# Two RG-LRU pairs around a chunked RWKV-7 recurrence: later places for convolutions, gate products and the second pair, state sums in PSUM, one square on ScalarE

## The chip, the core and the metric

The kernel runs on one core of a Trainium2 chip. The metric is the time of one execution on the device in microseconds, the median of several runs. One further execution is recorded by the hardware profiler; its rows are what the text below reads. Engines are named PE (TensorE; PEld its weight loads), DVE (VectorE), ACT (ScalarE), POOL (GpSimd) and SP (which here issues nearly all DMAs).

## The reference, cut to what matters

Two layers over 512 tokens and a model width of 1024. Each layer projects the normed input once and feeds three mixers, whose gated outputs are concatenated, projected and added to the residual. Two mixers matter here. RWKV-7 carries a 64 x 64 state per head (8 heads) along the tokens; the RG-LRU is a causal convolution of four taps, two gates from 64 x 64 blocks, and an elementwise linear recurrence. The third mixer, latent attention (MLA), follows after both.

```python
# rwkv7_mix, per token
sa = einsum('bhij,bhj->bhi', S, kk_t)
S = S * w_t[:, :, None, :] - sa[..., None] * b_t[:, :, None, :] + v_t[..., None] * k_t[:, :, None, :]
y_t = einsum('bhij,bhj->bhi', S, r_t)
# rglru_mix
xc = conv_b + sum(up[:, j:j + T] * conv_w[j] for j in range(4))
gate_r = sigmoid(xb @ ga_w + ga_b); gate_i = sigmoid(xb @ gx_w + gx_b)
log_a = -8.0 * gate_r * softplus(-lam); a = exp(log_a)
bx = sqrt(-expm1(2.0 * log_a)) * (gate_i * xc)
h_t = a_t * h_{t-1} + bx_t          # then rms_norm over the 512 channels
```

## The kernel before

Channels lie on the 128 partitions, tokens along the free axis, so each 512-wide mixer is four blocks of 128 channels. A projection block (`proj`, L331) is 24 matmuls of 128 x 128 x 512: fp32 weights and inputs are each split in two fp32r halves, and three of the four products are summed (`mm3`, L232). `weights` (L217) loads a raw half-block (`wr`, 3 buffers), ScalarE copies its high part (`wH`, 4 buffers), and VectorE or GpSimd subtracts to get the low part (`wL`, 4 buffers, L229): VectorE takes every `wmod`-th half, GpSimd the others. `wmod` is set by the stages; in the stretch of the change it is 2 (`WB`).

RWKV-7 is computed in eight chunks of 64 tokens (`chunk`, step `H`). Chunk `ch` multiplies the state by prepared matrices (L849, 16 matmuls into `ck`), adds the result to the values `UV` on VectorE (L852, two halves), multiplies values by keys (L859, 16 matmuls into `so` in PSUM), and makes the next state on VectorE: sum with the old state (L863), times the decay (L864); in chunk 0 only the product (L866). Every second chunk also makes outputs (L877, L883), copies them (L885, VectorE), squares them (L886, ScalarE) and reduces them (L887, VectorE). The eight chunks are a serial chain between TensorE and VectorE; matmuls of projections that don't depend on it can stand between its steps.

The RG-LRU blocks 0 and 1 are prepared before the chunks, 2 and 3 between them. `lru_a` (step `A`) projects a block, copies it with a margin (`ub`) and scales it (`xc`, L679) on ScalarE, adds three taps on VectorE (L681), multiplies by the gate blocks on TensorE (L687) and applies sigmoids and a tanh. `lru_b` (step `B`) takes a pair of blocks: exponential on ScalarE, `a` squared on GpSimd (L702), two VectorE operations (L704, L705), root on ScalarE, a product on GpSimd (L710), the scan on VectorE (L712), squares (L716, L718), their sum on GpSimd (L719), and the gated output on VectorE (L720). `B0` stands before the chunks, `B1` is called after them.

The order of calls is written by hand in strings (`ORD1` to `ORD3`). It is a priority, not the order on an engine: the framework plans each engine's fixed order of instructions ahead of time from the calls and from its own estimate of when operands are ready, so an instruction of a later call can stand before one of an earlier call. `act` (L133) chains all table functions of ScalarE in the order of the calls. Tiles of one tag share a fixed number of buffers: `g2` (128 x 512 floats) has 11, the projection accumulators `acc` four PSUM banks. After the chunks come `N0` (group norm), output gates `g`, latent projections `t` (four accumulators at once, `lat_products` L901), `T` (latents), `R0` (token sums of the RG-LRU, L379 on TensorE), `Y0` (split of its outputs), then output projections and attention.

Of the kernel before, what the change touches and what calls it, by code (L numbers as in the profile page):

```python
# [1 line left out]

# [9 lines left out]
AF = mybir.ActivationFunctionType  # L12
# [4 lines left out]
T = 512  # L17
# [30 lines left out]
def body(ctx, tc, x, wc, wl, wo, w2a2, gagx, wuq, wukv, vec, ln_g, fin_g, cst, out, depth=DEPTH):  # L48
# [11 lines left out]
    BN = (2, 2, 0, 0)  # L60
    ORD1 = "M0 L0 L1 C0 M1 C1 P0 L2 O0 M2 U1 O1 C2 U2 P1 L3 M3 C3 U0 P2 O2"
    ORD2 = "G0 U3 G1 P3 G2 Z0 Z1 O3 G3 X0 f4 V0 V1 Z2 Q0 Q1 f0 V2 V3 f1 Q2 Q3 J0 f2 J1 K0 f3 W0 K1 W1 f5 W2 W3"
    ORD3 = "B0 H0 H1 A2 H2 H3 A3 H4 H5 H6 H7 B1 N0 g0 g1 t0 t6 t1 t2 t4 t5 t3 t7 T0 R0 Y0 g2 g3 T1"
    LO = "0ig12uw3yvcm"
    Q1 = "aoooottttaaaooookvvqvkqvkqkqqqqq"
    WA, WB, WC, WD, WF = 1000, 2, 2, 5, 1000

    def tl(tag, shape, dt=F32, bufs=1):
        cnt[0] += 1
# [2 lines left out]
    def g2(shape=(128, 512)):  # L72
        return tl("g2", shape, F32, bufs=11)
# [16 lines left out]
    def ps(shape=(128, 512)):  # L90
        cnt[0] += 1
        return PS.tile(list(shape), F32, tag="ps", name=f"ps_{cnt[0]}", bufs=2)
# [40 lines left out]
    def act(out, in_, func, **kw):  # L133
        st = {AF.Sigmoid: "S", AF.Tanh: "S", AF.Sqrt: "Q"}.get(func, "E")
        if cur[0] != st:
            chained(A.preload_act_table_set(SETS[st]))  # L136
            cur[0] = st
        chained(A.activation(out=out, in_=in_, func=func, **kw))  # L138

    def copy(out, in_, **kw):  # L140
        i = A.activation(out=out, in_=in_, func=AF.Copy, **kw)  # L141
        return getattr(i, "ins", i)
# [178 lines left out]
    def one_layer(l):  # L321
        def vc(n, j):
            o = VO[n] + j
            return vecs[:, l, o:o + 1]
# [6 lines left out]
        def proj(j, halves=False):  # L331

            if halves:
                o = acc()
                W = [weights(wc[l, j, :, 4 * hf:4 * hf + 4, :].rearrange("p k c -> p (k c)"), raw=raws.pop((j, hf), None)) for hf in range(2)]
                for th in range(2):
                    t = slice(th * 256, (th + 1) * 256)
                    for k in range(8):
                        s = slice((k % 4) * 128, (k % 4 + 1) * 128)
                        w = W[k // 4]  # L340
                        mm3(o[:, t], (w[0][:, s], w[1][:, s]), (xH[:, k, t], xL[:, k, t]), k == 0, k == 7)
                return o
            o, parts = proj_parts(j)
            for part in parts:
                part()
            return o
# [320 lines left out]
        gw = tl("w2", [128, 2, 4, 64])  # L667
        nc.sync.dma_start(out=gw, in_=gagx[l])

        st = {}  # L670

        def lru_a(*js, o=None):
            for j in js:
                o = o or proj(17 + j)
                ub = g2([128, T + 3])
                G.memset(ub[:, 0:3], 0.0)
                copy(ub[:, 3:], o)
                xc = g2()
                A.activation(out=xc, in_=o, func=AF.Identity, scale=vc("cw", 12 + j), bias=vc("cb", j))  # L679
                for t in range(3):  # L680
                    V.scalar_tensor_tensor(out=xc, in0=ub[:, t:t + T], scalar=vc("cw", 4 * t + j), in1=xc, op0=ALU.mult, op1=ALU.add)  # L681
                gt = []
                for w in range(2):
                    o = ps()
                    for e in range(2):
                        hr = slice(64 * e, 64 * e + 64)
                        PE.matmul(o[hr, :], gw[hr, w, j, :], xc[hr, :], start=True, stop=True)  # L687
                    s = g2()
                    act(s, o, AF.Sigmoid, bias=vc("gx_b" if w else "ga_b", j))
                    gt.append(s)  # L690
                G.tensor_tensor(out=gt[1], in0=gt[1], in1=xc, op=ALU.mult)
                th = g2()
                act(th, gt[0], AF.Tanh, scale=sp8[:, l, j:j + 1])
                st[j] = (gt[0], gt[1], th)
                o = None

        def lru_b(*js):
            for j in js:
                a, bx, th = st[j]
                act(a, a, AF.Exp, scale=nsp8[:, l, j:j + 1])  # L700
                a2 = g2()
                G.tensor_tensor(out=a2, in0=a, in1=a, op=ALU.mult)  # L702

                V.scalar_tensor_tensor(out=a2, in0=a2, scalar=1.0, in1=th, op0=ALU.add, op1=ALU.mult)  # L704
                V.tensor_scalar(out=a2, in0=a2, scalar1=1.0e-34, scalar2=None, op0=ALU.max)  # L705
                st[j] += (a2,)
            for j in js:
                a, bx, th, a2 = st[j]
                act(a2, a2, AF.Sqrt)
                G.tensor_tensor(out=bx, in0=bx, in1=a2, op=ALU.mult)  # L710
                hs = th
                V.tensor_tensor_scan(out=hs, data0=a, data1=bx, initial=0.0, op0=ALU.mult, op1=ALU.add)  # L712
                sq = a2
                if j == 0:
                    stb[0] = tl("sqn", [128, T])
                    A.activation(out=stb[0], in_=hs, func=AF.Square)  # L716
                else:
                    A.activation(out=sq, in_=hs, func=AF.Square)  # L718
                    G.tensor_tensor(out=stb[0], in0=stb[0], in1=sq, op=ALU.add)  # L719
                V.scalar_tensor_tensor(out=hs, in0=hs, scalar=vc("out_g", j), in1=gz[j], op0=ALU.mult, op1=ALU.mult)  # L720
                yb.append(hs)
# [119 lines left out]
        def chunk(ch):  # L841
            cp, par = ch // 2, ch % 2
            ur = slice(64 * (1 - par), 64 * (1 - par) + 64)
            if ch:
                uo = [ck([128, 4, 64]) for _ in range(2)]
                for p in range(4):
                    for e in range(2):
                        hr = slice(64 * e, 64 * e + 64)
                        PE.matmul(uo[e][ur, p, :], AR[p][hr, 0, ch * 64:(ch + 1) * 64], S[ch][hr, p, :], start=True, stop=True)  # L849
                for e in range(2):  # L850
                    u = UV[ur, :, ch, 64 * e:64 * e + 64]
                    V.tensor_tensor(out=u, in0=uo[e][ur, :, :], in1=u, op=ALU.add)  # L852
            if ch < 7:
                so = ck([128, 4, 64])
                for p in range(4):
                    for e in range(2):
                        hr = slice(64 * e, 64 * e + 64)
                        hc = slice(e * 64, (e + 1) * 64)
                        PE.matmul(so[hr, p, :], BT[p][:, ch, hc], UV[:, p, ch, hc], start=True, stop=True)  # L859
                sn = S[ch + 1] = tl("S", [128, 4, 64], bufs=3)  # L860
                pc = PC[:, :, ch:ch + 1].to_broadcast([128, 4, 64])
                if ch:
                    V.tensor_tensor(out=sn, in0=so, in1=S[ch], op=ALU.add)  # L863
                    V.tensor_tensor(out=sn, in0=sn, in1=pc, op=ALU.mult)  # L864
                else:
                    V.tensor_tensor(out=sn, in0=so, in1=pc, op=ALU.mult)  # L866
            if par == 0:
                return
            yt = c2([128, 4, 2, 64])
            sq = c2([128, 4, 2, 64])  # L870
            yo = [ps([128, 4, 64]) for _ in range(2)]

            for p in range(4):
                for e, q in ((0, 0), (1, 1), (0, 1), (1, 0)):
                    hr, uq, c = slice(64 * e, 64 * e + 64), slice(64 * q, 64 * q + 64), 2 * cp + q
                    if c:
                        PE.matmul(yo[e][uq, p, :], AR[p][hr, 1, c * 64:(c + 1) * 64], S[c][hr, p, :], start=p == 0, stop=False)  # L877
            for e in range(2):
                hc = slice(e * 64, (e + 1) * 64)
                for p in range(4):  # L880
                    for q in range(2):
                        uq, c = slice(64 * q, 64 * q + 64), 2 * cp + q
                        PE.matmul(yo[e][uq, p, :], AM[q][:, p * 8 + e * 4 + cp, 64:128], UV[:, p, c, hc], start=c == 0 and p == 0, stop=p == 3)  # L883
            for e in range(2):
                V.tensor_copy(out=yt[:, :, e, :], in_=yo[e])  # L885
                A.activation(out=sq[:, :, e, :], in_=yo[e], func=AF.Square)  # L886
            V.tensor_reduce(out=vr[:, cp, :, :], in_=sq, axis=AX.X, op=ALU.add)  # L887
            yts.append(yt)
# [53 lines left out]
        def b_split(_):  # L942
            yb[:] = [ysplit(y) for y in yb]

        steps.update({"H": chunk, "N": lambda _: group_norm(), "A": lru_a, "B": lambda i: lru_b(2 * i, 2 * i + 1), "R": b_sums, "Y": b_split,
                      "t": lat_products, "T": latents, "g": lambda p: gzc.append(gate(25 + p))})
        run(ORD2)
        run(ORD3)
# [278 lines left out]
```

## Time and profile before

| | us |
|---|---|
| median of three runs (lowest, highest) | 849.87 (849.64, 851.14) |
| the profiled execution | 847.71 |
| its span, first to last instruction | 845.9 |

| engine | busy us | share of the span |
|---|---|---|
| PE | 791.7 | 94% |
| PEld | 619.4 | 73% |
| DVE | 538.9 | 64% |
| ACT | 519.3 | 61% |
| POOL | 353.3 | 42% |

A line such as L229 is the line of the kernel. A group is written as line, engine, operation, outputs <- inputs by the tiles' names. The releaser of a wait is what the profile shows as the last event before the waiting instruction could start. "Busy" of TensorE is modelled for pipelined matmuls. The chunks of layer 0 lie at about 201 to 258 us of the span, those of layer 1 at 615 to 672.

### The profile page before, as it was taken

The numbers are of one execution on the slowest core, as the hardware profiler recorded it, in microseconds if no ns is written. First come the engines' busy times: TensorE is split into PE (matmuls) and PEld (weight loads), VectorE is DVE, ScalarE is ACT, GpSimd is POOL, SyncE is SP. The second block draws the span as 40 slices with busy tenths as digits, with TensorE's granted clock in tenths as the row PEclk, the third lists the DMA queues.
The fourth block names the chain that finished last, engine by engine and source line by source line (L and its number), as shares of the span: only waits on it lengthen the run. The fifth ranks groups of instructions, "written<-read, shape, count | busy, mean of one in ns | idle before, by whom it ended". The sixth has DMA issues, their size and how long they took to land. (4 is left out here: it accounts for less than half of the span.)

```text
span 845.9 us, 15219 instructions
## 1 busy us (share of the span) xinstructions
PE 791.7 (94%) x5696; PEld 619.4 (73%) x5696; DVE 538.9 (64%) x1115; ACT 519.3 (61%) x1018; POOL 353.3 (42%) x321
## 2 busy tenths in 40 slices
PE   4999999999879999999989999999998799999995
PEld 3878888886659877657778788888765697775674
DVE  5678776924977364774474966695367953577636
ACT  5667875657563576664467687845666436765635
POOL 0455557522452455022344556574143425530323
PEclk9999999999998999999999999999999899999998
DMA  7222134311113375123732233332001234731354
GB/s 246 98 76 74 66 111 132 112 58 33 33 39 113 120 229 193 55 90 92 272 122 89 75 100 100 101 112 92 30 26 43 80 95 140 244 120 50 112 174 162
DMA packets 49754, 91.07 MB, mean 108 GB/s; under 512 B 5520, under 2 KB 8336, under 8 KB 49680
## 3 DMA queue, kind: packets, MB, share of 16 engines
q1 hardware_dynamic: 49104, 89.05, 32.8%
q8 instruction: 45, 0.74, 0.4%
q10 hardware_dynamic: 576, 1.05, 0.3%
q14 instruction: 29, 0.24, 0.1%
HBM read 73.30 MB, written 16.78 MB: 106 GB/s over the span
## 5 line engine op out<-in xcount | busy, mean ns | idle before, releaser
L229 POOL TENSOR_TENSOR wL<-wr,wH 128x512 fp32r<-128x512 f32 (+1 forms) x148 | 196.8, 1336 | 283.9 <-ACT wH L141 270.4
L141 ACT ACTIVATE wH<-wr 128x512 fp32r<-128x512 f32 (+1 forms) x192 | 118.8, 622 | 142.8 <-PE acc L234 73.9
L233 PE MATMUL acc<-xH,wH 128*128 128x512 f32 (+1 forms) x496 | 191.9, 388 | 0.0
L234 PE MATMUL acc<-xL,wH 128*128 128x512 f32 (+1 forms) x496 | 189.3, 382 | 0.7 <-DVE xL L306 0.6
L235 PE MATMUL acc<-xH,wL 128*128 128x512 f32 (+1 forms) x496 | 188.5, 380 | 0.0
L234 PEld LDWEIGHTS acc<-xL,wH 128*128 128x128 f32 x496 | 94.0, 190 | 17.5 <-DVE xL L306 1.4
L233 PEld LDWEIGHTS acc<-xH,wH 128*128 128x128 f32 x496 | 93.5, 189 | 18.1 <-ACT xH L141 0.7
L235 PEld LDWEIGHTS acc<-xH,wL 128*128 128x128 f32 x496 | 93.9, 189 | 17.2
L233 PE MATMUL acc<-wH,c 128*128 128x512 f32 x192 | 82.5, 430 | 0.1
L234 PE MATMUL acc<-wL,c 128*128 128x512 f32 x192 | 76.7, 399 | 0.0
L235 PE MATMUL acc<-wH,c 128*128 128x512 f32 x192 | 76.2, 397 | 0.0
L141 ACT ACTIVATE UV<-ps 64x512 f32<-64x512 f32 (+4 forms) x112 | 52.4, 494 | 28.8 <-PE ps L1076 22.0
L229 DVE TENSOR_TENSOR wL<-wr,wH 128x512 fp32r<-128x512 f32 (+1 forms) x44 | 32.6, 744 | 53.0 <-ACT wH L141 52.9
L138 ACT ACTIVATE c<-acc,sm 128x128 f32<-128x128 f32 (+3 forms) x64 | 33.6, 528 | 19.0 <-DVE sm L1060 19.0
L1058 PE MATMUL acc<-am,am 128*128 128x128 f32 (+3 forms) x128 | 42.8, 447 | 0.9 <-ACT c L138 0.8
L234 PEld LDWEIGHTS acc<-wL,c 128*128 128x128 f32 x192 | 36.5, 190 | 8.7 <-issue 1.9
L233 PEld LDWEIGHTS acc<-wH,c 128*128 128x128 f32 x192 | 36.3, 189 | 8.7 <-issue 2.2
L235 PEld LDWEIGHTS acc<-wH,c 128*128 128x128 f32 x192 | 36.3, 189 | 8.2 <-issue 0.5
L136 ACT ACT_TABLE_LOAD x31 | 39.8, 1283 | 1.3 <-PEq L1215 0.7
L138 ACT ACTIVATE g<-g 128x512 f32<-128x512 f32 (+1 forms) x58 | 36.4, 628 | 4.6 <-DVE g L705 2.6
L369 POOL TENSOR_TENSOR g<-g,g 128x512 f32<-128x512 f32 x24 | 32.2, 1340 | 13.9 <-ACT g L138 13.9
L141 ACT ACTIVATE c<-g 128x512 fp32r<-128x512 f32 (+1 forms) x40 | 24.9, 629 | 18.8 <-DVE g L980 7.2
(219 smaller groups left out, 1587.7 us busy)
## 6 DMA issues: line engine op xcount, KB each, us to landing
wr<-in_wc_dram SPq DMA_DIRECT2D x116, 256.0 KB, 2.7
wr<-in_wo_dram SPq DMA_DIRECT2D x48, 256.0 KB, 3.4
hp<-dr SPq DMA_DIRECT2D x38, 256.0 KB, 3.5
dr<-hp SPq DMA_DIRECT2D x28, 256.0 KB, 3.3
dr<-g SPq DMA_DIRECT2D x16, 256.0 KB, 2.5
g<-dr SPq DMA_DIRECT2D x16, 256.0 KB, 3.5
wr<-in_wl_dram SPq DMA_DIRECT2D x16, 208.0 KB, 2.5
dr<-c SPq DMA_DIRECT2D x12, 256.0 KB, 3.7
```

The source lines that it names most:

```text
L136: chained(A.preload_act_table_set(SETS[st]))
L138: chained(A.activation(out=out, in_=in_, func=func, **kw))
L141: i = A.activation(out=out, in_=in_, func=AF.Copy, **kw)
L229: (V if wn[0] % wmod[0] == 0 or wn[0] <= 4 else G).tensor_tensor(out=L, in0=raw, in1=f(H), op=ALU.subtract)
L233: PE.matmul(o, a[0], b[0], start=start, stop=False)
L234: PE.matmul(o, a[0], b[1], start=False, stop=False)
L235: PE.matmul(o, a[1], b[0], start=False, stop=stop)
L369: G.tensor_tensor(out=z, in0=z, in1=s, op=ALU.mult)
L1058: PE.matmul(o[:, 0:n], qT[:, hd, qt * 128:n], K2[:, p, e, 0:n], start=True, stop=True)
```

## The change

`lru_a` is cut in three: `lru_in` (projection, copy, scaling), `lru_conv` (the three taps on VectorE) and `lru_gates` (gate matmuls, sigmoids, product, tanh). Blocks 0 and 1 still run all three in a row. For blocks 2 and 3 the steps are placed one by one: input, `c2`/`c3` for the taps and `a2`/`a3` for the gates. `tc.issue_after(x)` puts an ordering edge from each instruction traced inside it to `x`, if both are on the same engine: the taps' VectorE instructions come behind the last value update L852 traced so far, the gates' matmuls behind the last L859 traced so far, and the VectorE instructions of `B1` behind the L852 of chunk 7. Instructions on other engines get no edge. The new `WE` makes `wmod` 1000 from `B0` on, so that until the latent projections set it again every half's low part is made on GpSimd. `a` is squared on ScalarE, and the state sum is written in place in PSUM and multiplied out of it.

```diff
-    ORD3 = "B0 H0 H1 A2 H2 H3 A3 H4 H5 H6 H7 B1 N0 g0 g1 t0 t6 t1 t2 t4 t5 t3 t7 T0 R0 Y0 g2 g3 T1"
+    ORD3 = "B0 H0 H1 A2 H2 c2 H3 A3 a2 H4 c3 H5 a3 H6 H7 B1 N0 g0 g1 t0 t6 t1 t2 t4 t5 t3 t7 T0 R0 Y0 g2 g3 T1"
-    WA, WB, WC, WD, WF = 1000, 2, 2, 5, 1000
+    WA, WB, WC, WD, WE, WF = 1000, 2, 2, 5, 1000, 1000
...
+        def lru_a(j, o=None):
+            lru_in(j, o)
+            lru_conv(j)
+            lru_gates(j)
+
+        def lru_in_chain(j):
+            wmod[0] = WE
+            lru_in(j)
+
+        def conv_behind(j):
+            with tc.issue_after(mark["V"]):
+                lru_conv(j)
+
+        def gates_behind(j):
+            with tc.issue_after(mark["P"]):
+                lru_gates(j)
+
+        def lru_b_behind(i):
+            wmod[0] = WE
+            with tc.issue_after(mark["V"]) if i else nullcontext():
+                lru_b(2 * i, 2 * i + 1)
...
                 a2 = g2()
-                G.tensor_tensor(out=a2, in0=a, in1=a, op=ALU.mult)
+                A.activation(out=a2, in_=a, func=AF.Square)
...
-                    V.tensor_tensor(out=u, in0=uo[e][ur, :, :], in1=u, op=ALU.add)
+                    mark["V"] = V.tensor_tensor(out=u, in0=uo[e][ur, :, :], in1=u, op=ALU.add).ins
...
-                        PE.matmul(so[hr, p, :], BT[p][:, ch, hc], UV[:, p, ch, hc], start=True, stop=True)
+                        mark["P"] = PE.matmul(so[hr, p, :], BT[p][:, ch, hc], UV[:, p, ch, hc], start=True, stop=True).ins
...
                 if ch:
-                    V.tensor_tensor(out=sn, in0=so, in1=S[ch], op=ALU.add)
-                    V.tensor_tensor(out=sn, in0=sn, in1=pc, op=ALU.mult)
-                else:
-                    V.tensor_tensor(out=sn, in0=so, in1=pc, op=ALU.mult)
+
+                    V.tensor_tensor(out=so, in0=so, in1=S[ch], op=ALU.add)
+                V.tensor_tensor(out=sn, in0=so, in1=pc, op=ALU.mult)
...
-        steps.update({"H": chunk, "N": lambda _: group_norm(), "A": lru_a, "B": lambda i: lru_b(2 * i, 2 * i + 1), "R": b_sums, "Y": b_split,
+        steps.update({"H": chunk, "N": lambda _: group_norm(), "A": lru_in_chain, "c": conv_behind, "a": gates_behind, "B": lru_b_behind, "R": b_sums, "Y": b_split,
```

## Rows read from the trace of the kernel before

**Rows 1.** The page, busy time by engine: us, share of the span, instructions.
```profile
PE 791.7 (94%) x5696; PEld 619.4 (73%) x5696; DVE 538.9 (64%) x1115; ACT 519.3 (61%) x1018; POOL 353.3 (42%) x321
```

**Rows 2.** Waits of TensorE, whole span: us in total, times, longest.
```profile
PE ck L849 <- DVE S L864: 9.2, 6, 3.1
PE ps L883 <- DVE UV L852: 5.3, 7, 1.6
PE ps L687 <- DVE g L681: 4.2, 2, 2.1
```

**Rows 3.** Busy us of PE, PEld, DVE, ACT, POOL, then granted clock, DMA, GB/s.
```profile
208.00:259.00 51.00, 41.94 (x544) 31.15 (x545) 42.65 (x67) 29.42 (x47) 24.08 (x20) 0.94 0.19 58
253.50:259.60 6.10, 5.74 (x82) 5.03 (x83) 4.97 (x9) 1.85 (x4) 1.14 (x1) 0.50 0.55 200
637.80:641.20 3.40, 3.38 (x20) 1.27 (x22) 3.17 (x6) 1.25 (x2) 0.00 (x0) 0.64 0.49 125
670.50:673.90 3.40, 3.33 (x33) 2.94 (x34) 2.31 (x6) 0.97 (x3) 0.00 (x0) 0.50 0.28 101
```

**Rows 4.** Timeline of TensorE: start, us, line, operands, count [idle before, releaser].
```profile
215.84 0.68 PE L849 MATMUL ck<-S,c 64*64 64x64 f32 x16 [1.24 <-DVE S L864]
...
224.31 1.93 PE L687 MATMUL ps<-g,w 64*64 64x512 f32 x8 [2.10 <-DVE g L681]
...
241.86 0.57 PE L883 MATMUL ps<-UV,am 128*64 128x64 f32 x12 [1.60 <-DVE UV L852]
...
253.56 0.80 PE L849 MATMUL ck<-S,c 64*64 64x64 f32 x10 [3.13 <-DVE S L864]
...
670.57 1.97 PE L883 MATMUL ps<-UV,am 128*64 128x64 f32 x30 [1.27 <-DVE UV L852]
```

**Rows 5.** Timeline of VectorE, layer 0: start, us, line, operands, count [idle before].
```profile
214.76 0.69 DVE L704 SCALAR_TENSOR_TENSOR g<-g,g 128x512 f32<-128x512 f32 x1 [0.87 <-POOL g L676]
215.37 0.42 DVE L864 TENSOR_TENSOR S<-S,PC 128x256 f32<-128x256 f32 x1
...
239.97 1.51 DVE L704 SCALAR_TENSOR_TENSOR g<-g,g 128x512 f32<-128x512 f32 x1 [1.47 <-POOL g L702]
...
247.16 3.44 DVE L712 TENSOR_TENSOR_SCAN g<-g,g 128x512 f32<-128x512 f32 x2
...
252.03 1.48 DVE L864 TENSOR_TENSOR S<-S,PC 128x256 f32<-128x256 f32 x1
253.43 2.42 DVE L720 SCALAR_TENSOR_TENSOR g<-g,vecs,g 128x512 f32<-128x512 f32 x2
```

**Rows 6.** Lines L863, L864, L866: count, ns min/median/max, first and last start.
```profile
L863 DVE TENSOR_TENSOR S<-ck,S x12: 406/425/425, 212.0 to 665.0; 128x256 f32<-128x256 f32 x12
...
L864 DVE TENSOR_TENSOR S<-S,PC x12: 412/613/1478, 215.4 to 666.4; 128x256 f32<-128x256 f32 x12
...
L866 DVE TENSOR_TENSOR S<-ck,PC x2: 424/424/425, 208.1 to 621.5; 128x256 f32<-128x256 f32 x2
```

**Rows 7.** Lines L681, L1059, L229, the same view.
```profile
L681 DVE SCALAR_TENSOR_TENSOR g<-g,vecs,g x24: 718/752/1754, 188.8 to 645.3; 128x512 f32<-128x512 f32 x24
...
L1059 DVE TENSOR_TENSOR acc<-acc,cmask x64: 273/290/300, 334.9 to 795.0; 128x128 f32<-128x128 f32 x64
...
L229 POOL TENSOR_TENSOR wL<-wr,wH x148: 1072/1294/1801, 29.6 to 825.0; 128x512 fp32r<-128x512 f32 x140, 128x416 fp32r<-128x416 f32 x8
...
L229 DVE TENSOR_TENSOR wL<-wr,wH x44: 579/689/1230, 12.6 to 827.1; 128x512 fp32r<-128x512 f32 x36, 128x416 fp32r<-128x416 f32 x8
```

**Rows 8.** Groups by shape, 208 to 260 us: busy us, mean ns, idle before.
```profile
L681 DVE SCALAR_TENSOR_TENSOR g<-g,vecs,g 128x512 f32<-128x512 f32 x6 | 6.1, 1016 | 0.0
...
L702 POOL TENSOR_TENSOR g<-g 128x512 f32<-128x512 f32 x4 | 5.1, 1284 | 1.5 <-ACT g L138 1.4
...
L718 ACT ACTIVATE g<-g 128x512 f32<-128x512 f32 x3 | 1.9, 631 | 3.1 <-DVE g L712 3.1
```

**Rows 9.** Timeline of TensorE, 274 to 300 us.
```profile
277.81 0.95 PE L379 MATMUL ck<-ones,sqn 128*128 128x2 f32 x8
```

More of the change, by code (lines that the diff above doesn't have):

```diff
@@ L1 @@
-from contextlib import ExitStack
+from contextlib import ExitStack, nullcontext
 import concourse.bass as bass
@@ L668, in one_layer @@
         nc.sync.dma_start(out=gw, in_=gagx[l])
[L670 to L695, printed above, removed]
@@ new lines, in one_layer, with lru_in, lru_conv @@
+        st, mark = {}, {}
+        def lru_in(j, o=None):
+            o = o or proj(17 + j)
+            ub = g2([128, T + 3])
+            G.memset(ub[:, 0:3], 0.0)
+            copy(ub[:, 3:], o)
+            xc = g2()
+            A.activation(out=xc, in_=o, func=AF.Identity, scale=vc("cw", 12 + j), bias=vc("cb", j))
+            st[j] = ub, xc
+        def lru_conv(j):
+            ub, xc = st[j]
+            for t in range(3):
+                V.scalar_tensor_tensor(out=xc, in0=ub[:, t:t + T], scalar=vc("cw", 4 * t + j), in1=xc, op0=ALU.mult, op1=ALU.add)
@@ new lines, in lru_gates @@
+        def lru_gates(j):
+            xc, gt = st[j][1], []
+            for w in range(2):
+                o = ps()
+                for e in range(2):
+                    hr = slice(64 * e, 64 * e + 64)
+                    PE.matmul(o[hr, :], gw[hr, w, j, :], xc[hr, :], start=True, stop=True)
+                s = g2()
+                act(s, o, AF.Sigmoid, bias=vc("gx_b" if w else "ga_b", j))
+                gt.append(s)
+            G.tensor_tensor(out=gt[1], in0=gt[1], in1=xc, op=ALU.mult)
+            th = g2()
+            act(th, gt[0], AF.Tanh, scale=sp8[:, l, j:j + 1])
+            st[j] = (gt[0], gt[1], th)
```

## The prediction

> **What bounds the kernel now.** Read the busy shares first: TensorE is busy in 94% of the span [rows 1]. Where it works without a gap nothing beside it counts, so the second view is who TensorE waited for. Three waits of this kernel belong to the edited stretch, the eight chunks of the recurrence, once in each layer: the state update before the next chunk's first products (9.2 us in 6 waits), the value update before the output products (5.3 us in 7), and the convolution before the RG-LRU gates (4.2 us in 2), together 18.7 us [rows 2]. All three name VectorE. The third view is busy time by stretch: in layer 0, from 208 to 259 us, VectorE is busy 42.65 of 51 us, so the chain's small operations often stand behind others. [...] Then the timelines of TensorE and VectorE are laid side by side, to see which operation stood in front of which wait [rows 4, 5].
>
> **The change, part by part.**
>
> *Second pair's recurrences behind the chain (B1).* In layer 0 TensorE waits 1.60 us at 241.86, 3.13 us at 253.56 and 0.30 us once more for chunk 7's update; layer 1 repeats this with 1.60, 3.11 and, at 670.57, 1.27 [rows 2, 4]. In front of the first stands L704 of the second pair (1.51 us). In front of the second stand its two scans (3.44 us) and a state update stretched to 1.48 us; in front of the third its two L720 (2.42 us) [rows 5]. Under the change all second-pair VectorE work comes after chunk 7's value update, so these go: 5.0 + 6.0 = 11.0 us, and the two slow stretches that begin there, 2.9 + 1.7 = 4.5 us.
> The moved work isn't free: L704 at 1.51 and, as at 214.76, 0.69; scans 3.44; L720 2.42; and two L705, which have no row here and are priced as L704, 1.38: 9.4 us of VectorE after the chain [rows 5]. It hides if its readers are late. The nearest is the token sums L379 on TensorE, at 277.81 [rows 9], 22 us after chunk 7's value update, which starts when the L720 of 253.43 end (255.85) [rows 5]. The tail is those 9.4 us plus a root and a square at L718's 0.63 and a GpSimd product and sum at 1.28 [rows 8]: 13.2 us. Priced at 0. With the cover gone, 13.2 us a layer at worst.
>
> *Convolutions and gate products later.* The two waits before L687 (2.10 at 224.31 [rows 4], as much in layer 1; 4.2 us [rows 2]) and the layer-1 slow stretch behind one of them (1.2 us) go, because the products now come a chunk after their convolution. The convolutions stay in the chain: three per block, six per layer, each 0.718 to 1.754 us [rows 7], 6.1 us for the six of layer 0 [rows 8]. Each may stand in front of a chain operation, as L704 stands directly before the state update L864 at 214.76 and 215.37 [rows 5]. Bounds: nothing, if the fill matmuls of the next projections cover them; 6.1 us a layer if every one is exposed. I take half, 3.0 us a layer, since both cases stand in the trace: TensorE runs fill beside some convolutions and waits for others.
>
> *State sums in PSUM.* L863 (one SBUF operand, one PSUM) took 406 to 425 ns in all twelve cases; L864 (both operands SBUF) 412 to 1478 ns; L866, which multiplies out of PSUM as the new L864 will, 424 ns in both of its cases [rows 6]. So the new L864 is 424 to 425 ns, 12 ns over the best old case and 1.05 us under the worst. The in-place sum into PSUM isn't in the trace in this shape; the nearest is L1059, 128 x 128 in place, 290 ns [rows 7]; at the 1.2 ns a column that lie between the best L864 (256 columns, 412 ns) and the best L681 (512 columns, 718 ns), 128 columns more make 0.44 us, no change. Its upper bound is twice the 290 ns, 0.58. Bounds for the pair: -1.05 to +0.2 us per chunk. What it saves is inside waits already counted, above all the 1.48 us operation before the 3.13 us wait.
> [...]
>
> *a squared on ScalarE.* It takes 1.28 us operations, L702, from GpSimd and adds 0.63 us ones, as L718 runs [rows 8], four per layer. For the first pair it lets L704 run earlier, and so L864 at 215.37, behind which TensorE waits 1.24 us at 215.84 [rows 4, 5]. That wait goes in both layers, 2.5 us. ScalarE is not full there; 0.63 us each is hidden, at worst 0.6 us in front of a value copy.
>
> *Weight halves.* The new modulus sends all halves of the blocks and of the first two output gates to GpSimd: 1.29 us instead of 0.69 [rows 7], two per layer that run in the chain. They queue in order behind products that wait for ScalarE. Bounds: 0 to 2 x 1.29 = 2.6 us a layer; I take 1.2, the longer run time alone.
>
> *The small waits*, what is left of the 18.7 (1.0 us), are each a chain operation late by a fraction: counted as removed, with 0.9 us a layer of new ones in their place. Slow clock after new waits: 0.8 us a layer.
>
> **The sum.** Removed: 11.0 + 4.2 + 2.5 + 1.0 = 18.7, and 5.8 of clock: 24.5. Put back: 2 x (3.0 + 1.2 + 0.9 + 0.8) = 11.8. Net 12.7 us. The profiled execution took 847.7 us (span 845.9): 835.0. The median shown is 2.2 us above that execution: 837.2 us.
>
> **Rivals.**
>
> *A. The convolutions take the place of what leaves.* All six exposed (6.1), a gate wait of 2.1 left, the halves at 2.6, and the 0.9 and 0.8: 12.5 us a layer, 25 in all with every bound reached. With three quarters to nine tenths of that, 18.8 to 22.5, the gain is 2 to 6: 844 to 848 us. For: L681 reached 1.754 us, and GpSimd gets more halves. Against: some 9 us of VectorE leave the chain in each layer.
>
> *B. Given back.* The lat products after the chain could be limited by their weights, so that TensorE gets there earlier and waits: gain 0 to 2, time 848 to 850. Against: none of the waits of rows 2 names a weight.
>
> *C. Slower: the tail holds the buffers.* The second pair keeps a, bx, th and a-squared twice (8 of 11 g2 buffers), two gates of it 2 more, and one output gate the 11th. The second output gate then can't leave its accumulator until a scan has freed a buffer, and the four latent accumulators need all four banks. In layer 0 the pair takes from 239.97, its first VectorE operation, to 250.60, the end of its scans: 10.6 us [rows 5]. If no latent products are planned into that stretch, TensorE waits it out, and a slow stretch of 2.9 us follows: 13.5 us a layer, 27.0 against the 24.5 removed: 852 us. It decides from 12.2 us a layer on. For: the buffers do count up to 11. Against: behind chunk 5, where the last gate products are put, two chunks and output gates still stand in TensorE's queue.
>
> *D. Near all of it goes:* 2 us a layer put back, gain 20.5, time 829.
>
> **How the numbers follow.** Forecast 0.60 (gain 6 to 20), A below that 0.14, B 0.08, C 0.12, D 0.06. About 0.2% (1.7 us) is what a measurement can tell from no change here. Faster: 0.60 + 0.14 + 0.06 = 0.80; same 0.08 (B); slower 0.12 (C). The range 829 to 848 leaves out C, part of B and the edge of D, under 0.2; the forecast's own is 830 to 844.
>
> **What would show it.** Right: no second-pair VectorE operation (second L704, L712, L720 pair) before chunk 7's L852; waits of TensorE on L864 and L852 down from 14.5 us to under 6; L864 at 424 ns throughout; no 0.50 clock at the end of the chunks; L687 without a 2 us wait; latent products starting 4 to 9 us earlier in each layer. Wrong: new waits on L681, on wL of GpSimd, or on the accumulators (L141 copies) before the first latent products; TensorE waiting at L379. The prediction fails above all if the planned order of VectorE still puts convolutions between sum and product of every chunk.

## The result, and the profile after

The changed kernel takes 856.64 us (median of 4 runs, 855.67 to 858.33), against 849.75 us before (4 runs): a ratio of 1.0083 (95% interval 1.0060 to 1.0106), 7 us slower. 837.2 us was forecast, with a range of 829 to 848. The profiled execution took 856.39 us (span 854.6), 8.7 us more than the 847.7 (span 845.9) of before. Of two experiments below, e5 and x7, the profiled execution ran at a granted clock of 0.56 and 0.848, so their medians leave it out and their traces are not read.

First the page's busy times, to be set beside [rows 1], then the waits of TensorE (total us, times, longest), beside [rows 2]. L864 of before is now L892, L852 is L879, L681 is L685.

```profile
PE 795.1 (93%) x5696; PEld 622.9 (73%) x5696; DVE 545.2 (64%) x1107; ACT 521.7 (61%) x1026; POOL 353.4 (41%) x321
```

```profile
PE acc L233 <- ACT g L141: 8.7, 2, 4.4
PE ck L876 <- DVE S L892: 6.7, 6, 2.2
PE ck L886 <- DVE UV L879: 5.3, 6, 1.7
...
PE ps L693 <- DVE g L685: 1.6, 2, 0.8
...
PE acc L234 <- DVE wL L229: 1.4, 2, 0.9
```

The three waits of before, 18.7 us, have become 13.6 us in the chunks (6.7 + 5.3 + 1.6; for the value update it is now the products of values and keys, L886, that wait, where before it was the output products), and two stand beside them: 8.7 us in which the first latent products (L233) wait for an accumulator that ScalarE's copy L141 has not emptied, and 1.4 us for a weight half. Together 23.7, that is 5.0 more. The same matrix work also kept TensorE busy 3.4 us longer (795.1 against 791.7), at a lower mean granted clock (0.978 against 0.984). 5.0 + 3.4 = 8.4 of the 8.7 us.

Where it falls shows in the busy time by stretch (columns as in [rows 3]) and in TensorE's timeline of layer 0 (start, us, line, operands, count, idle before), to be set beside [rows 4]:

```profile
208.00:256.40 48.40, 42.73 (x550) 31.89 (x549) 36.33 (x61) 27.10 (x45) 16.70 (x14) 0.93 0.14 41
256.40:272.00 15.60, 10.38 (x42) 9.44 (x41) 15.32 (x22) 7.75 (x13) 9.08 (x8) 0.78 0.25 76
226.50:233.50 7.00, 5.81 (x111) 5.39 (x111) 4.78 (x9) 1.87 (x4) 1.27 (x1) 0.52 0.15 40
262.50:267.80 5.30, 5.24 (x15) 5.01 (x16) 5.16 (x6) 2.48 (x6) 4.46 (x4) 0.51 0.39 121
```

```profile
216.19 0.51 PE L876 MATMUL ck<-S,c 64*64 64x64 f32 x10 [1.02 <-DVE S L892]
...
226.77 0.80 PE L876 MATMUL ck<-S,c 64*64 64x64 f32 x10 [2.13 <-DVE S L892]
...
262.56 0.71 PE L233 MATMUL acc<-wH,xH 128*128 128x416 f32 x1 [4.36 <-ACT g L141]
271.32 0.46 PE L234 MATMUL acc<-wL,xH 128*128 128x416 f32 x1 [0.85 <-DVE wL L229]
```

Up to the chunks' end the change gains: the first latent products start at 256.36, 3.2 us earlier than the 259.58 of before. After nine of them TensorE stops for 4.36 us. From 256.4 to 272 it is busy 10.38 of 15.6 us, and VectorE, with the pair's work, 15.32. The granted clock is 0.51 for 5.3 us behind that wait. Busy time times the missing share puts its cost at 5.24 x 0.49 = 2.6 us, an estimate; the latent products follow each other at 0.35 us there, at 0.19 us after it. The clock is also 0.52 for 7 us behind the 2.13 us wait of chunk 3 (5.81 x 0.48 = 2.8 us, estimated likewise). So the slow stretch at the end of the chunks (0.50 [rows 3]) is gone from layer 0, as forecast (1.00 from 233.5 to 256.4 us), and two new ones stand in other places.

Who is late at 262.56 is read from ScalarE's timeline:

```profile
253.55 0.60 ACT L141 ACTIVATE g<-acc 128x512 f32<-128x512 f32 x1
...
257.70 0.63 ACT L745 ACTIVATE g<-g 128x512 f32<-128x512 f32 x1 [2.59 <-DVE g L739]
...
261.39 0.63 ACT L745 ACTIVATE g<-g 128x512 f32<-128x512 f32 x1 [1.12 <-DVE g L739]
261.93 0.58 ACT L141 ACTIVATE g<-acc 128x512 f32<-128x512 f32 x1
```

The first output gate leaves its accumulator at 253.55. The second gate's products are complete when the latent products begin, at 256.36, but its copy runs only at 261.93: ahead of it in ScalarE's order stand the squares L745 of the second pair's two scans, and these wait for VectorE. ScalarE sat idle for 1.12 us before the second square, with the copy's input long complete: it keeps its planned order. VectorE's timeline of the same time, and of the stretch before the 2.13 us wait, with GpSimd's below:

```profile
220.75 2.83 DVE L685 SCALAR_TENSOR_TENSOR g<-g,vecs,g 128x512 f32<-128x512 f32 x2
223.50 1.77 DVE L747 SCALAR_TENSOR_TENSOR g<-g,vecs,g 128x512 f32<-128x512 f32 x1
225.30 0.43 DVE L891 TENSOR_TENSOR ck<-ck,S 128x256 f32<-128x256 f32 x1
225.64 0.74 DVE L685 SCALAR_TENSOR_TENSOR g<-g,vecs,g 128x512 f32<-128x512 f32 x1
226.30 0.42 DVE L892 TENSOR_TENSOR S<-ck,PC 128x256 f32<-128x256 f32 x1
...
249.01 0.75 DVE L879 TENSOR_TENSOR UV<-ck,UV 64x256 f32<-64x256 f32 x2 [1.33 <-PE ck L876]
...
255.38 2.29 DVE L739 TENSOR_TENSOR_SCAN g<-g,g 128x512 f32<-128x512 f32 x1
...
260.15 1.21 DVE L739 TENSOR_TENSOR_SCAN g<-g,g 128x512 f32<-128x512 f32 x1
```

```profile
219.58 1.74 POOL L229 TENSOR_TENSOR wL<-wr,wH 128x512 fp32r<-128x512 f32 x1 [0.58 <-ACT wH L141]
221.28 1.75 POOL L746 TENSOR_TENSOR sqn<-sqn,g 128x512 f32<-128x512 f32 x1
222.98 1.73 POOL L229 TENSOR_TENSOR wL<-wr,wH 128x512 fp32r<-128x512 f32 x1
```

The pair's scans come after chunk 7's value update (L879 at 249.01), as the change says. Ahead of chunk 3, two convolutions and a first-pair product (the gated output L747) take 2.83 + 1.77 us in front of the sum L891, and a third convolution stands between that sum and its product L892. From 219.58 to 224.71 GpSimd runs two weight halves and the first pair's sum of squares (L746) without a gap, each at 1.73 to 1.75 us, and there VectorE's convolutions (1.42 us each) and L747 (1.77 us) are long; the convolution at 225.64, after them, took 0.74.

### The profile page after: what moved, and what is told of

Read it like the earlier page. It is cut to its first block, busy times and chain, and to the rows that moved or that the text cites. A ratio compares the mean times of both kernels' runs of the same rounds, so it can differ in the third digit from the quotient of the medians.

```text
span 854.6 us, 15199 instructions
## 1 busy us (share of the span) xinstructions
PE 795.1 (93%) x5696; PEld 622.9 (73%) x5696; DVE 545.2 (64%) x1107; ACT 521.7 (61%) x1026; POOL 353.4 (41%) x321
## 5 line engine op out<-in xcount | busy, mean ns | idle before, releaser
L229 POOL TENSOR_TENSOR wL<-wr,wH 128x512 fp32r<-128x512 f32 (+1 forms) x156 | 207.8, 1338 | 286.2 <-ACT wH L141 282.9
L141 ACT ACTIVATE wH<-wr 128x512 fp32r<-128x512 f32 (+1 forms) x192 | 118.9, 622 | 133.8 <-PE acc L234 71.1
L233 PE MATMUL acc<-xH,wH 128*128 128x512 f32 (+1 forms) x496 | 192.0, 388 | 0.0
L233 PEld LDWEIGHTS acc<-xH,wH 128*128 128x128 f32 x496 | 94.5, 191 | 18.0 <-ACT xH L141 0.7
L233 PE MATMUL acc<-wH,c 128*128 128x512 f32 x192 | 82.3, 429 | 0.2 <-DVE c L461 0.2
L141 ACT ACTIVATE UV<-ps 64x512 f32<-64x512 f32 (+4 forms) x112 | 52.4, 494 | 28.8 <-PE ps L1102 22.0
L229 DVE TENSOR_TENSOR wL<-wr,wH 128x512 fp32r<-128x512 f32 (+1 forms) x36 | 27.2, 755 | 30.6 <-ACT wH L141 30.6
L233 PEld LDWEIGHTS acc<-wH,c 128*128 128x128 f32 x192 | 36.1, 188 | 8.8 <-issue 1.8
L141 ACT ACTIVATE c<-g 128x512 fp32r<-128x512 f32 (+1 forms) x40 | 24.9, 629 | 24.4 <-DVE g L747 12.4
```

What stands on the lines that cost most here:

```text
L229: (V if wn[0] % wmod[0] == 0 or wn[0] <= 4 else G).tensor_tensor(out=L, in0=raw, in1=f(H), op=ALU.subtract)
L233: PE.matmul(o, a[0], b[0], start=start, stop=False)
```

## The experiments

All ratios are to the kernel before, run on the same chip; times are medians, and the interval is 95%. Two edited kernels are compared by their medians; between the series the median of the kernel before went from 849.30 to 849.88, so half a microsecond between them means nothing. "The latent wait" below is that of the first latent products (L233) for the second output gate's copy, and "the queue" is ScalarE's planned order, in which that copy has its place.

**Is it the tie, the buffers, or the order?** e1 leaves out the tie of the pair to chunk 7:

```diff
-            with tc.issue_after(mark["V"]) if i else nullcontext():
+            with nullcontext():
                 lru_b(2 * i, 2 * i + 1)
```


> The changed kernel with one part undone: the second pair's VectorE work is no longer tied behind chunk 7. Theory 'buffer' (the second output gate's copy waits for one of the 11 g2 buffers, which the late pair holds, and the four accumulators of the latent products wait for that copy): the 4.4 us wait of TensorE before the latent products, one in each layer, goes, and the waits on L852/L864 that the pair caused come back, some 11 us with slow clock 4 us: 852 to 858 us in all. Theory 'convolutions' (the loss is made by the taps and gate products among the chunks, the pair's place matters little): 855 to 858 us, and the waits inside the chunks are the same as in the changed kernel.

857.06 us, 1.0093 (1.0075 to 1.0110); no change against the changed kernel, and the 8.7 us wait stays. With the gate products late, the pair comes behind the chunks by itself: its first VectorE operation (L731) starts at 249.97, after chunk 7's value update at 248.31.

e2 is the kernel before with the pair's recurrences behind chunk 7, and nothing else:

```diff
+        def lru_b_behind(i):
+            with tc.issue_after(mark["V"]) if i else nullcontext():
+                lru_b(2 * i, 2 * i + 1)
```


> The kernel before with one part of the change alone: the second pair's VectorE work behind chunk 7. Theory 'buffer': the waits of 1.6, 3.1 and 0.3 to 1.3 us inside the chunks go (11.0 us, 4.5 us of clock), and a wait of about 4 us before the latent products comes in each layer with some 2.5 us of slow clock: 848 to 852 us. Theory 'convolutions': no new wait of this size, so about 838 us.

844.29 us, 0.9945 (0.9931 to 0.9960): 5.2 us faster, between the two expectations. The latent wait is here too, 5.4 us, but the chain's waits of 14.5 us [rows 2] are down to about 4.

```profile
PE acc L233 <- ACT g L141: 5.4, 2, 2.7
```

e3 gives the pair's two squares their own place, so that two more gate buffers are free:

```diff
-                a2 = g2()
+                if j == 2:
+                    big = c8([128, 2, T])
+                a2 = g2() if j < 2 else big[:, j - 2, :]
```


> The changed kernel, but the second pair's two squares lie in the c8 buffer, which is idle there, so that two more g2 buffers are free; nothing else differs. Theory 'buffer': the second output gate is copied right after its last product, the 4.4 us wait and the half clock behind it go in both layers: 856.6 - 8.7 - 5 = 843 us. Rival 'queue' (the copy stands on ScalarE behind the pair's squares, whatever the buffers): the wait stays, 855 to 857 us.

856.51 us, 1.0089 (1.0073 to 1.0106), with the same 8.7 us wait (longest 4.4).

So the buffers do not hold the copy, as the rival has it. e4 leaves the buffers and writes the two output gates ahead of the pair:

```diff
-    ... H6 H7 B1 N0 g0 g1 t0 ...
+    ... H6 H7 g0 g1 B1 N0 t0 ...
```


> The changed kernel with the output gates g0 and g1 called before the second pair, so that they get their buffers and their places on ScalarE first. Theories 'buffer' and 'queue': the wait before the latent products goes, 841 to 846 us; the pair ends some 3 us later, which nothing waits for. Theory 'convolutions': 854 to 857 us.

850.80 us, 1.0011 (0.9997 to 1.0024): 5.8 us faster than the changed kernel, and yet outside both expectations, 841 to 846 and 854 to 857. The 8.7 us wait is gone, the chain's waits are where they were (6.8, and 5.3 at L886), and 3.1 us have come up at the token sums L379:

```profile
PE ck L876 <- DVE S L892: 6.8, 6, 2.2
...
PE ck L379 <- POOL sqn L746: 3.1, 2, 1.6
```

So the latent wait is the order on ScalarE: more buffers leave it, and writing the gates' calls first, which puts their copies ahead of the pair's work, takes it away. (Their work on other engines moves with them.) It is not the whole loss: the chunks' waits stay, and behind the wait at L379 (the sums start at 277.3 us) the granted clock is lower than before it: its mean is 0.97 from 208 to 275 us and 0.95 from 200 to 300.

**The late convolutions and gate products.** e7 has them alone; e11 is the changed kernel without them; e9 has sums and square alone; x1 is e2 with the output gates first.

```diff
# e7: the kernel before with
+    ORD3 = "B0 H0 H1 A2 H2 c2 H3 A3 a2 H4 c3 H5 a3 H6 H7 B1 N0 g0 g1 ...
# e11: the changed kernel with
-    ORD3 = "B0 H0 H1 A2 H2 c2 H3 A3 a2 H4 c3 H5 a3 H6 H7 B1 N0 g0 g1 ...
+    ORD3 = "B0 H0 H1 A2 H2 H3 A3 H4 H5 H6 H7 B1 N0 g0 g1 ...
# e9: the kernel before with
+                A.activation(out=a2, in_=a, func=AF.Square)
+                    V.tensor_tensor(out=so, in0=so, in1=S[ch], op=ALU.add)
# x1: e2 with
+    ORD3 = "... H7 g0 g1 B1 N0 t0 ...
```


> The kernel before with one part of the change: the second pair's convolutions and gate products stand later among the chunks (c2, a2, c3, a3); the second pair is not tied behind the chain, a is squared on GpSimd, the state sums stay in SBUF and the weight halves keep their split. Theory (the late convolutions and gate products are the loss: the gates come so late that the pair lands behind the chunks and the second output gate's copy waits behind it): 855 to 860 us, with the wait of the first latent products for L141 there, over 3 us a layer. Rival 1 (the loss needs the parts together, above all the square on ScalarE, which stands in the queue of that copy): 846 to 851, latent wait under 1 us a layer. Rival 2 (the weight halves on GpSimd are the loss): 844 to 849.

848.61 us, 0.9995 (0.9978 to 1.0012). The theory that the late place is a loss in itself falls: alone it changes nothing that can be measured. The latent wait that it named did come, 10.6 us, and the waits of [rows 2] are down by about 9: by making the pair late it does what the tie does, and pays the same queue.

```profile
PE acc L233 <- ACT g L141: 10.6, 2, 5.3
```

> The changed kernel with one part undone: each second-pair block runs its convolutions and gate products at once, as before; the pair stays tied behind chunk 7, the square on ScalarE, the sums in PSUM, the halves on GpSimd. Theory (the late convolutions and gate products are the loss): 838 to 845 us, chain waits (L892 and L879 together) under 5 us, waits for gate inputs of 4 us back. Rival 1 (square on ScalarE and sums carry part of the loss): 847 to 852, with the latent wait over 3 us a layer. Rival 2 (the halves on GpSimd are the loss): 853 to 858, that is no change against the changed kernel.

850.40 us, 1.0012 (0.9998 to 1.0027). 6 us of the loss go, some 9 us of expected gain do not come; rival 1 gave the time, but the latent wait is 2.9 us a layer, just under the 3 that it asked for, and the wait that grew is another:

```profile
PE ps L693 <- DVE g L685: 9.3, 4, 3.8
PE acc L233 <- ACT g L141: 5.8, 2, 2.9
```

The convolutions, in their old place, are late by 3.84 us instead of 2.10 [rows 4], beside weight halves on GpSimd that were not all there before (three from 218.98 to 226.3 us, where one ran before). That put the halves under suspicion.

> The kernel before with two small parts of the change: the state sums in PSUM and a squared on ScalarE; pair, convolutions, gates and halves as before. Theory (these two are nearly free and help a little: the update behind which the chain waits is no longer stretched): 845 to 849 us, chain waits (state and value update) under 10 us instead of 14.5. Rival (the square on ScalarE stands in front of the copies and takes the gain back): 850 to 853.

845.53 us, 0.9956 (0.9940 to 0.9972): 3.8 us faster, a time as expected; the chain's waits (6.5 at L849, 2.5 at L881 and 1.3 at L859) are 10.3 us, just over the 10 that were expected.

> The kernel before with the second pair's recurrences behind chunk 7 and, in the written order, the two output gates ahead of that pair, so that their copies stand in front of the pair's work on ScalarE. Theory (with the pair alone behind the chain, 844.3 us, the 5.4 us wait of the latent products is the queue of ScalarE, and goes): 838 to 842. Rival 1 (the pair is then late for the token sums L379, which take the place of the wait): 843 to 846. Rival 2 (the wait was buffers, not the queue): 843 to 846 with the latent wait still there.

845.42 us, 0.9948 (0.9929 to 0.9967): no gain over e2. The latent wait goes, 3.1 us come at L379 and 2.2 at weight halves from GpSimd, so what it gave is given back, as rival 1 has it.

**The weight halves and the square.** In the next four, e8 is the changed kernel with the halves split again, e12 is e11 with them split, e13 is the changed kernel with the square on GpSimd, and x2 is x1 with the sums in PSUM.

```diff
# e8, e12
-    WA, WB, WC, WD, WE, WF = 1000, 2, 2, 5, 1000, 1000
+    WA, WB, WC, WD, WE, WF = 1000, 2, 2, 5, 2, 1000
# e13
-                A.activation(out=a2, in_=a, func=AF.Square)
+                G.tensor_tensor(out=a2, in0=a, in1=a, op=ALU.mult)
# x2: x1 with
+                    V.tensor_tensor(out=so, in0=so, in1=S[ch], op=ALU.add)
```


> The changed kernel with one part undone: the weight halves of the second pair's blocks and of the first output gates are split between VectorE and GpSimd again (WE = 2 in place of 1000). Theory H (GpSimd's extra halves are a part of the loss: they delay GpSimd's products, on which scans and squares wait, and stretch VectorE's two-operand work): 848 to 853 us. Rival (the halves don't matter, the loss is the late convolutions meeting the tied pair): 855 to 858.

852.15 us, 1.0032 (1.0019 to 1.0044): 4.5 us better than the changed kernel, as theory H has it. VectorE's order is another here (the sum L891 stands before the first-pair product L747, and no convolution between sum and L892), and the product is a little shorter (1.64 us instead of 1.77); TensorE waits 1.19 instead of 2.13 us behind it:

```profile
221.08 0.43 DVE L891 TENSOR_TENSOR ck<-ck,S 128x256 f32<-128x256 f32 x1
221.43 1.64 DVE L747 SCALAR_TENSOR_TENSOR g<-g,vecs,g 128x512 f32<-128x512 f32 x1
222.99 0.41 DVE L892 TENSOR_TENSOR S<-ck,PC 128x256 f32<-128x256 f32 x1
```

```profile
PE acc L233 <- ACT g L141: 12.5, 2, 6.3
...
PE ck L876 <- DVE S L892: 3.5, 6, 1.2
PE ps L909 <- DVE UV L879: 2.8, 2, 1.4
```

The chunks' waits fell from 13.6 to 7.1 us (the third is 0.8 at L886), and the latent wait rose by 3.8: of the 6.5 us that the chunks gain, the queue takes more than half.

> The pair behind the chain, the square on ScalarE and the sums in PSUM together, with convolutions, gate products and weight halves as in the kernel before. Theory H (with the halves on GpSimd this was 850.4, and they are what took the gain): 838 to 843 us, the wait for gate inputs back from 9.3 to about 4.5. Rival 1 (square and pair get in each other's way on ScalarE: one part's gain excludes the other's): 844 to 848 with the latent wait above 2.5 us a layer. Rival 2 (halves don't matter): 849 to 852.

844.20 us, 0.9936 (0.9913 to 0.9960): 6.2 us better than with the halves on GpSimd, the wait for gate inputs back at 4.8 us as theory H has it, but the latent wait of 2.6 us a layer is that of rival 1, and so is the time. Both hold in part.

> The changed kernel with a squared on GpSimd again. Theory (the four squares on ScalarE, 0.63 us each, are a small part of the queue in front of the second output gate's copy, and helped the first pair): 856 to 860 us, the latent wait between 3.5 and 5 us a layer. Rival (the square on ScalarE is the loss): 848 to 853 with that wait under 2.5 us a layer.

866.38 us, 1.0199 (1.0180 to 1.0219): 10 us slower than the changed kernel, more than expected, with 5.2 us of latent wait a layer. Of the parts undone one by one (the tie in e1, the late place in e11, the halves in e8, the square here), the square on ScalarE is the only one whose loss makes the changed kernel slower.

> The kernel before with the second pair behind chunk 7, the two output gates written ahead of it, and the state sums in PSUM. Theory (the sums take the last stretched state update out of the chain, worth 1 to 2 us a layer, and nothing takes its place): 841 to 844 us. Rival (what is left in the chain is hidden or given back at the token sums L379): 845 to 847.

845.84 us, 0.9961 (0.9946 to 0.9977), as x1 and as the rival has it: the sums add nothing there.

**What was still open: the interaction.** x5 is e8 with the output gates first, x4 is e12 with them first, x6 is x4 with convolutions at once and gate products one chunk later, x7 is x4 with the token sums one gate later.

```diff
# x5 and x4: e8 and e12 with
-    ... H7 B1 N0 g0 g1 t0 ...
+    ... H7 g0 g1 B1 N0 t0 ...
# x6
+    ORD3 = "B0 H0 H1 A2 H2 a2 H3 A3 H4 a3 H5 H6 H7 g0 g1 B1 N0 t0 ...
             lru_in(j)
+            lru_conv(j)
# x7: x4 with
-    ... T0 R0 Y0 g2 g3 T1
+    ... T0 g2 R0 Y0 g3 T1
```


> The changed kernel with the weight halves split as before (that alone: 852.2) and the two output gates written ahead of the second pair. Theory Q (with convolutions and gates late, the pair is on ScalarE just when the second output gate's copy is due; the 12.5 us wait of the latent products is the whole price of the late place): 841 to 846 us, that wait under 2 us, with some 3 us at the token sums L379. Rival (the late place also costs elsewhere, clock and chain; as much comes back at L379): 847 to 851.

839.22 us, 0.9889 (0.9862 to 0.9916): 12.9 us faster than e8, below the 841 to 846 expected. ScalarE empties the second gate's accumulator at 252.54, ahead of all the pair's work, which begins with the two exponentials (the row with nsp) at 255.16:

```profile
252.54 0.58 ACT L141 ACTIVATE g<-acc 128x512 f32<-128x512 f32 x1
253.22 0.63 ACT L138 ACTIVATE g<-g 128x512 f32<-128x512 f32 x1
...
255.16 1.34 ACT L138 ACTIVATE g<-g,nsp 128x512 f32<-128x512 f32 x2
```

```profile
PE ck L876 <- DVE S L892: 3.4, 5, 1.2
PE ck L379 <- POOL sqn L746: 3.1, 2, 1.6
PE ps L909 <- DVE UV L879: 2.8, 2, 1.4
```

> Pair behind the chain, square on ScalarE, sums in PSUM, convolutions, gate products and weight halves as in the kernel before (that: 844.2), and the two output gates written ahead of the pair. Theory Q: the 5.3 us wait of the latent products goes, 3.1 us come at L379: 840 to 843 us. Rival (given back wholly, as it was without square and sums, where the same move changed 844.3 to 845.4): 844 to 846.

843.29 us, 0.9929 (0.9905 to 0.9953): 0.3 us above the range of theory Q, with the waits that it named (none of the latent products, 3.1 us at L379), and within 1 us of e12, so nearly all is given back. By the medians it is 4 us above x5, which would make the late place of convolutions and gates a gain once the queue is out of the way; the intervals overlap, so this is not shown.

> As the run with early gates and the output gates first, but each second-pair block runs its convolutions at once and its gate products one chunk later (a2 after H2, a3 after H4), so that the products find their input ready without the convolutions moving. Theory (only the gate products' wait, 4.8 us, needed a later place; the convolutions did not): 836 to 841 us, wait for gate inputs under 1 us. Rival (the later gate products make the pair later, and the token sums L379 wait by as much): 841 to 846.

840.25 us, 0.9894 (0.9872 to 0.9917), as the theory has it. The gate wait is gone (no row for it is left), 5.4 us stand before L887 instead, which waits for the value update L880; level with x5.

> As the run with early gates and the output gates first, with the token sums L379 written one output gate later (T0 g2 R0 Y0 g3 T1). Theory (L379 waits for GpSimd's last square of the pair, 3.1 us, and a gate's products cover that): 837 to 840.5 us, no wait at L379. Rival (what follows the sums is then late by as much): 841 to 844.

843.44 us, 0.9928 (0.9902 to 0.9955), level with x4, so the rival holds as far as the time tells; whether L379's wait went is open.

**Sums and square by themselves.** e5 and e6 are the kernel before with one of e9's two edits each.

> The kernel before with the state sums in PSUM alone. Theory (the stretched state update goes from 1.48 us to 0.42, but in front of the 3.1 us wait the second pair's scans stay): 847 to 849.5 us. Rival (sums carry most of the 3.8 us that sums and square gave together): 845 to 847.

848.51 us, 0.9985 (0.9972 to 0.9998), as expected.

> The kernel before with a squared on ScalarE alone. Theory (the square lets the first pair's VectorE work start earlier, the wait of 1.24 us before the state update of layer 0's chunk 2 goes, in both layers): 846 to 848 us. Rival (the square alone gives nothing, the sums carried the 3.8 us): 848.5 to 851.

840.60 us, 0.9897 (0.9877 to 0.9917): 9 us faster, outside both expectations, and more than the sums and the square together. VectorE's rows at chunk 7 show one reason: in e6 the state update L864 stands before the second scan,

```profile
246.27 0.42 DVE L863 TENSOR_TENSOR S<-ck,S 128x256 f32<-128x256 f32 x1
...
247.69 0.41 DVE L864 TENSOR_TENSOR S<-S,PC 128x256 f32<-128x256 f32 x1
248.03 2.29 DVE L712 TENSOR_TENSOR_SCAN g<-g,g 128x512 f32<-128x512 f32 x1
```

and in e9, with the sums in PSUM as well, behind it, so that TensorE waits 3.17 us where in e6 it waits 0.68 (e6 pays a part back at the next value update, 2.74 us against 1.26):

```profile
251.46 0.43 DVE L863 TENSOR_TENSOR ck<-ck,S 128x256 f32<-128x256 f32 x1
252.61 2.26 DVE L712 TENSOR_TENSOR_SCAN g<-g,g 128x512 f32<-128x512 f32 x1 [0.72 <-POOL g L710]
254.80 0.39 DVE L864 TENSOR_TENSOR S<-ck,PC 128x256 f32<-128x256 f32 x1
```

**The whole in one table** (medians, us; all with pair behind, square and sums):

| | convolutions, gates early | late |
|---|---|---|
| halves split, pair first | 844.2 | 852.2 |
| halves split, output gates first | 843.3 | **839.2** |
| halves on GpSimd, pair first | 850.4 | **856.6** (the change) |
| halves on GpSimd, output gates first | (not run) | 850.8 |

From the change to the best kernel run are two edits: the halves split again, 4.5 us (11.6 once the gates are first), and the output gates written first, 12.9 us (5.8 with the halves on GpSimd). Together they give 17.4 us, and x5 beats both kernels. That x5 is better than e6, x6 or x4 the intervals do not tell: e6, a change of one line, gets as far. Writing the gates first paid where the latent wait was long, 4.4 us a layer (the change) or 6.3 (e8); where it was 2.6 or 2.7 (e12 to x4, e2 to x1) the time stayed within 1.2 us. The halves on GpSimd by themselves, on the kernel before, were not run.

## Why the prediction was wrong

Two steps failed. The first is the tail of the moved pair: "The nearest is the token sums L379 on TensorE, at 277.81 ... Priced at 0." The pair's results do have no reader before L379. But the pair puts eight operations on ScalarE (two exponentials, two squares, two roots, two squares of scans), with waits for VectorE between them, and behind these, in ScalarE's planned order, stands the copy which empties an accumulator that TensorE needs for the latent products. It is due at 256.36, 21 us before the 277.81. The term at 0 cost 8.7 us of waits, and slow clock behind them (by the estimate above 2.6 us in layer 0; in layer 1, from 681 to 687 us at 0.50, 5.42 x 0.50 = 2.7). Moving the gates ahead took 5.8 us from the change (e4) and 12.9 from e8 (x5). Rival C had named the copy as the point of failure, at 852 us, but for want of buffers; e3 gave buffers and changed nothing. The prediction had also named both signs, waits for accumulators before the latent products and a convolution between sum and product; both are in the rows above.

The second is the weight halves, below. With both put right, x5 takes 839.22 us, within the range. In the sum for the profiled execution (835.0 forecast, 856.4 measured, 21.4 us apart) the latent wait is 8.7, a weight half 1.4, the waits in the chunks 3.4 (13.6 where 2 x (3.0 + 1.2 + 0.9) = 10.2 were put back), and TensorE's busy time 7.6 (up by 3.4 where 5.8 - 1.6 = 4.2 were to go): 21.1.

- *Pair out of the chain, 11.0 us:* right. No second-pair operation stands before chunk 7's update in the rows above; in e2 the chain's waits fall by 10.4 us, 5.4 of them go to the latent wait, and 5.2 are gained.
- *Weight halves, 1.2 us a layer:* too small, and the second failure. Three pairs of kernels give 4.5 (e8), 6.2 (e12) and 11.6 us (x5) for both layers, against 2.4 put back and 5.2 at the upper bound. The forecast counted the longer run time, not that beside three GpSimd operations in a row a convolution takes 1.42 us, where it took 0.74 after them, nor that VectorE's order changes.
- *Convolutions, 3.0 us a layer:* about the right size with the halves split (all chunk waits of x5 together are 7.0 us in both layers), not with the halves on GpSimd (13.6). The half was a choice between two bounds, so this is in part luck. Their written place does put one between sum and product, as was named as a failure.
- *Waits for gate inputs, 4.2 us:* 1.6 are left; right for most of it.
- *Square, 2.5 us:* far too low. Alone it gives 9.0 us and within the change 9.7 (e13); in e6 a part of that is VectorE's order, which was not priced, beside the wait at 215.84, which was. In the change that wait is still 1.02 us, in e6 and e8 0.16; between the change and e8 only the halves differ.
- *Sums in PSUM:* as forecast; below the convolutions and the new L892 by shape (busy us, mean ns): 14 products at 419 ns on average (409 to 426), where L864 reached 1478 [rows 6].

```profile
L685 DVE SCALAR_TENSOR_TENSOR g<-g,vecs,g 128x512 f32<-128x512 f32 x24 | 24.3, 1013 | 1.8 <-POOL g L676 1.1
...
L892 DVE TENSOR_TENSOR S<-ck,PC 128x256 f32<-128x256 f32 x14 | 5.9, 419 | 1.8 <-PE ck L886 1.6
```

- *Slow clock, 5.8 us removed and 1.6 put back:* no run shows the 5.8 us; they are an estimate from the last three lines of [rows 3] (clocks of 0.50, 0.64 and 0.50), busy time times the missing share: 5.74 x 0.50 + 3.38 x 0.36 + 3.33 x 0.50 = 2.9 + 1.2 + 1.7. In the changed kernel's trace slow clock came back behind the new waits (0.52 behind the 2.13 us, 0.51 behind the 4.36 us; 2.8 and 2.6 us by the same estimate), and TensorE's busy time is up by 3.4 us.

The sum also added its terms. Alone, the pair is worth 5.2, the square 9.0, the sums 1.1 and the late place 0.7 (not clear of nothing), some 16 us. Square and sums together give 3.8, with the pair 5.1, with the late place they lose 2.9, and with the halves on GpSimd 7. The pair and the late place take away the same waits and fill the same queue, and the edits rearrange VectorE's order for one another, as e6 against e9 and e8 against the change show. How much of each fall is order and how much is longer operations was not told apart.

## What to carry to other kernels

When work is moved behind a chain, look in each engine's order, not only in the data, for who comes after it: the copy out of an accumulator that stands behind a waiting operation comes after it too, and here it was due first. Write such copies ahead of the moved work, and see what is due next: here the token sums, 3.1 us, gave back a short wait whole. And price work for GpSimd by how long VectorE's operations take beside it (here 1.42 us a convolution, 0.74 after it), not by its own length alone.

## What the runs showed of the hardware that was not expected

In proportion, small operations of VectorE stretched most here: L918 took 7 times what the same operation took before, where the longest state update took 3.6 times the shortest (412 to 1478 ns [rows 6]) and the longest convolution 2.4 times (718 to 1754 ns [rows 7]). The group norm's root works on 128 x 32 elements; in the changed kernel it stands beside GpSimd's work on the pair, the output gates and the weight halves, and L202 took 859 ns on average (six), where it took 320 before; L918 took 1280 ns, and L892 of before, which is the same operation, 182. In the kernel before it was another of them, L199, that took 1154 ns (170 in the changed kernel). L918 and L199 read one tile, so operations with one input were not spared either. The same trace has both cases: L202 took 1.19 us while GpSimd was busy, and 0.18 after GpSimd had stopped at 266.96. So an operation of 0.2 us took as long as a GpSimd operation of 128 x 512 (1.28 us).

```profile
L202 DVE SCALAR_TENSOR_TENSOR vr<-vr,vr 128x32 f32<-128x32 f32 x6 | 5.2, 859 | 0.1
...
L918 DVE TENSOR_SCALAR vr<-vr 128x32 f32<-128x32 f32 x2 | 2.6, 1280 | 0.0
```

```profile
261.28 1.19 DVE L202 SCALAR_TENSOR_TENSOR vr<-vr,vr 128x32 f32<-128x32 f32 x1
...
267.82 0.18 DVE L202 SCALAR_TENSOR_TENSOR vr<-vr,vr 128x32 f32<-128x32 f32 x1
```

And the executions of x5 differ with the clock that they were granted: six took 838.65 to 845.5 us at mean clocks of 0.996 down to 0.982, the lower the clock, the longer the time.
